# Inter-chunk output of a Mamba-2 scan: from a scaled PSUM product to C multiplied by the decays on GpSimd, accumulated in place

## The chip, the cores and the metric

The kernel runs on one core of a Trainium2 chip. The metric is the device time of one execution in microseconds; three runs of the kernel before took 2874.92, 2874.94 and 2874.92 us (median 2874.92). Five engines work side by side, each through its own queue in program order: PE (matmuls), DVE (vector), ACT (scalar activations), POOL (GpSimd) and SP (which here only issues transfers). Matmuls write PSUM; DVE and ACT read PSUM and write SBUF.

## What is computed

One layer of a hybrid decoder on 256 prompt tokens and 64 sample tokens (T = 320 columns): a SwiGLU feed-forward block, a token mixer, and a second feed-forward block. The mixer holds a state-space scan in chunks of 128 tokens, and the change is inside it:

```
cum      = cumsum(dt * A)                       # per chunk and head
y_diag   = (C B^T * exp(cum_t - cum_s) * dt) x  # within a chunk
h_start  = state at the chunk's start           # chunk 0: zero; chunk 1: from chunk 0
y_off[t] = exp(cum_t) * (C_t . h_start)         # from the earlier chunk
y        = y_diag + y_off + D * x
```

There are 32 heads of 64 channels in four groups of eight; a group shares B and C (128 states). The prompt has two chunks, so y_off exists for tokens 128 to 255 alone. The state at the prompt's end, exp(cum_end) * h_start plus chunk 1's own sum, is an output too (o_hp). The mixer further has a 31-tap depthwise convolution with a layer norm, three kinds of gates on the projection's columns, a norm over the scan's output and two output projections.

## The kernel before, in words

**The main stream.** Every dense layer goes through `phase` (line 328). Weights stream from HBM in tiles of 128 x 512 (a chunk holds four 128 x 128 blocks). Each is split into a high part on ACT (wh) and a low part on DVE (wl), and each block takes three matmuls of 320 columns: wh by the high input, wl by the high input, wh by the low input. The input projection's second part, `WIN_2`, has 40 groups of two column blocks; a group runs 32 block steps, so 96 matmuls, into two PSUM banks named acc. There are four such banks. `WIN_PLAN` (line 50) gives the kind of each group: eight "x" groups feed the scan, "z" groups gate its output, "gcc" and "gssd" groups are gates, "glu" groups feed the 31-tap convolution. When a group ends, a small task reads its two banks out and thereby frees them.

**What orders the rest.** All side work is written as Python generators that a planner interleaves with the main stream while the program is built; the queues then execute in the order that came out. One tick is two block steps, so six main matmuls. At each tick `step_bg` (line 296) lets generators go on while its estimates of the DVE and ACT clocks are less than 1.4 us ahead of its PE clock. A generator says `yield n` to sleep n ticks; LAG is 5. If the main stream needs a PSUM bank that is not free, `force` (line 306) moves the tasks and the generators of priority below 3, without regard to sleeping, and with no main matmul written in between, until the bank is free.

**The scan.** `ssd` (line 815) goes through the four groups. For a group it transposes x and B, makes `xdt` (x times dt) and `xw` (x times the decays to the chunk's end), the masked product of B and C (`cbm`), and `s0`, the state after chunk 0. Then (lines 1013 to 1027) it waits LAG ticks, takes two banks named m (there are three), multiplies C by s0 on PE into one bank and sums chunk 1's state into the other; DVE scales the first by exp(cum) into `yo1`, scales s0 by the chunk's decay, adds the sum, and POOL stores s0 to o_hp.

Next come two halves of four heads; a half is called a pair p, 0 to 7. `load_w` has broadcast the pair's cum rows from a DRAM scratch, `cumd`, to all partitions of `wd` (two buffers: one in tile eu, one in the last four slices of x). The generator waits until 12 ticks after that load was issued; ACT subtracts (12 Relu activations of 128 or 64 columns) and takes the exponential, DVE multiplies by cbm, and LAG + 3 ticks later PE forms y for the pair in two m banks: xdt by wd for three token blocks, plus yo1 by the identity for chunk 1, plus the sample part by a selection matrix. DVE adds D * x, y is ready, and `load_w(p + 2)` is issued LAG ticks later.

**What waits for the scan.** After the last pair of group 3 and the few instructions behind it, the generator says "ypath" (line 1087). `gate1` (line 1197) for blocks 12 to 15 and `gate2` (line 1202) hold back until then, since they write where wd and the scan's tiles lie: the two "gcc" groups behind the "z" groups, groups 29 and 30 of 40, leave their four acc banks occupied until "ypath". `sst` (line 920) updates the sample states, 32 tiles h0, and has POOL store each to o_hs; `conv31` (line 1092) runs the long convolution on DVE and at the end of each of eight channel blocks has POOL store a pad tile and load the next into the same buffer.

In the profile all PE, DVE and ACT instructions have the helper's line, L78, so they are told apart by their tiles. There fu holds xdt, s0 and yo1; gu holds xw; eu holds cbm, the transposed B and one wd; x is the other wd; hu and xb the sample state's inputs; bc is B and C; cw the constants with the identity. PE in 32-bit floating point shows two instructions for one matmul of the program.

Of the kernel before, what the change touches and what calls it, by code (L numbers as in the profile page):

```python
# [6 lines left out]
F32 = mybir.dt.float32  # L7
F32R = mybir.dt.float32r
AF = mybir.ActivationFunctionType
ALU = mybir.AluOpType  # L10
# [13 lines left out]
LAG = 5  # L24
# [145 lines left out]
class Builder:  # L170
# [432 lines left out]
    def mixer(self, on_k):  # L603
        nc, io = self.nc, self.io
# [10 lines left out]
        ident, ones = self.ident, self.ones  # L615
# [85 lines left out]
        ec1 = self.sp.tile([128, 32], F32, name="ec1", tag="ec1")  # L701
# [4 lines left out]
        def dt_gen(a):  # L706
            du = unit("du", "E")
            v = lambda i: du[0:32, i, :]
            V = nc.vector
# [26 lines left out]
            for i, cst in enumerate((13, 11, 9, 7, 5, 3)):  # L736
                V.scalar_tensor_tensor(v(1), v(1), 1.0 / cst, v(3), op0=ALU.add, op1=ALU.mult)
                if i % 3 == 2:
# [11 lines left out]
            cum, ec, dw = v(5), v(6), v(7)  # L750
# [9 lines left out]
            yield 1  # L760
            V.tensor_tensor(dw, dw, v(4), op=ALU.mult)
            nc.sync.dma_start(out=self.cumd, in_=cum)
            nc.scalar.activation(stg.rearrange("p (j i) -> p j i", i=32)[:, :, 0:16],
                                 ec[:, 256:320].rearrange("p (j i) -> p j i", i=16), AF.Copy)
            d1 = v(0)[:, 0:32]
# [18 lines left out]
            for e in range(2):  # L784
                nc.tensor.matmul(b2.ap[64 * e : 64 * e + 64, 64:192],
                                 lhsT=self.par[:, e : e + 1].to_broadcast([32, 64]),
                                 rhs=v(1)[:, 0:128], start=True, stop=True)
# [27 lines left out]
        def ssd():  # L815
# [6 lines left out]
            ef, ff, gf, hf = (q.rearrange("p a b -> p (a b)") for q in (eu, fu, gu, hu))  # L822
            wds = (eu[:, 0:4], self.x[:, 12:16])
            btok = ef[:, 1280:1664]
            cbm = ef[:, 1664:1984]
            yos = ef[:, 1984:2496]
            xdt = ff[:, 0:1536].rearrange("p (c f) -> p c f", c=3)
            s0 = ff[:, 1536:2048]
            yo1 = ff[:, 2048:2560]
            xw = gf[:, 0:1024].rearrange("p (c f) -> p c f", c=2)  # L830
            xws = gf[0:64, 1024:1536]
            xss = hf[0:96, 0:1024].rearrange("p (q f) -> p q f", q=2)
# [3 lines left out]
            V = nc.vector  # L836
            hd = lambda ap: ap.rearrange("p (h q) -> p h q", q=64)
            BLK = ((0, 0, 128), (1, 128, 128), (2, 256, 64))
            at = {}
            h0s = {}  # L840

            def tbc(i, c, g, n=128):
                return tk[0:n, i, c, 8 * g : 8 * g + 8].unsqueeze(2).to_broadcast([n, 8, 64])
# [12 lines left out]
            def load_w(p):  # L856
                if p < 8:
                    nc.sync.dma_start(out=wds[p % 2],
                                      in_=self.cumd[4 * p : 4 * p + 4].partition_broadcast(128))
                    at["w", p] = self.tick  # L860

            def load_h0(i):
                if i < 32:
                    g, q, jj = i // 8, i // 4 % 2, i % 4
                    h = self.hp.tile([128, 512], F32, name="h0", tag="h0")
                    nc.sync.dma_start(out=h, in_=io["h0"][4 * g + jj, q])
                    h0s[i] = h
                    at["h", i] = self.tick
# [80 lines left out]

            bhl = self.sp.tile([64, 2, 128], F32R, name="bhl", tag="bhl")  # L950
            load_w(0)
            assert "spilled" in self.ready
            load_w(1)
            self.spawn(sst_all(), 2.5)
            for i in range(3):
                load_h0(i)
            self.spawn(ysamp(), 1.5)
            for g in range(4):
# [3 lines left out]
                B, C = Bt(g), Ct(g)  # L962

                def xT(c):
                    _, t0, n = BLK[c]
                    b = self.ring("m")
                    for i in range(4):
                        nc.tensor.transpose(b.ap[0:n, 128 * i : 128 * i + 128], XS(4 * g + i)[:, t0 : t0 + n], ident)
                    return b
# [9 lines left out]
                b0, b1 = xT(0), xT(1)  # L979
# [7 lines left out]
                b0 = xT(2)  # L987
                b1 = self.ring("m")
# [10 lines left out]
                b0 = self.ring("m")  # L999
                b1 = self.ring("m")  # L1000
                nc.tensor.matmul(b1.ap, lhsT=btok[:, 0:128], rhs=xw[:, 0], start=True, stop=True)
                for c, t0, n in BLK:
                    nc.tensor.matmul(b0.ap[0:n, t0 : t0 + n], lhsT=B[:, t0 : t0 + n], rhs=C[:, t0 : t0 + n],
                                     start=True, stop=True)
# [3 lines left out]
                                op=ALU.mult)  # L1008
# [1 line left out]
                b0.free = True  # L1010
                nc.scalar.activation(s0, b1.ap, AF.Copy)
                b1.free = True
                yield LAG
                while not self.can("m", 2):
                    yield 1
                b0 = self.ring("m")
                b1 = self.ring("m")
                nc.tensor.matmul(b1.ap, lhsT=btok[:, 128:256], rhs=xw[:, 1], start=True, stop=True)
                nc.tensor.matmul(b0.ap, lhsT=C[:, 128:256], rhs=s0, start=True, stop=True)
                yield 1  # L1020
                V.tensor_tensor(hd(yo1), hd(b0.ap), tbc(2, 1, g), op=ALU.mult)
                b0.free = True
                V.tensor_tensor(hd(s0), hd(s0), ec1[:, 8 * g : 8 * g + 8].unsqueeze(2).to_broadcast([128, 8, 64]),
                                op=ALU.mult)
                V.tensor_tensor(s0, s0, b1.ap, op=ALU.add)
                b1.free = True
                nc.gpsimd.dma_start(out=io["o_hp"][g], in_=s0)
                yield 0
                for half in range(2):
                    p = 2 * g + half  # L1030
                    wd = wds[p % 2]
                    while ("w", p) not in at or self.tick < at["w", p] + 12:
                        yield 1
                    for i in range(4):
                        h = 4 * p + i
                        for c, t0, n in BLK:
                            nc.scalar.activation(wd[0:n, i, t0 : t0 + n], wd[0:n, i, t0 : t0 + n], AF.Relu,
                                                 bias=tk[0:n, 0, c, h : h + 1], scale=-1.0)
                        yield 0
                    nc.scalar.activation(wd[:, :, 0:256], wd[:, :, 0:256], AF.Exp, scale=-1.0)  # L1040
                    nc.scalar.activation(wd[0:64, :, 256:320], wd[0:64, :, 256:320], AF.Exp, scale=-1.0)
                    yield 2
                    V.tensor_tensor(wd[:, :, 0:256], wd[:, :, 0:256],
                                    cbm[:, 0:256].unsqueeze(1).to_broadcast([128, 4, 256]), op=ALU.mult)
                    V.tensor_tensor(wd[0:64, :, 256:320], wd[0:64, :, 256:320],
                                    cbm[0:64, 256:320].unsqueeze(1).to_broadcast([64, 4, 64]), op=ALU.mult)
                    yield LAG + 3
                    while ("yos", g) not in self.ready or not self.can("m", 2):
                        yield 1
                    bb = []  # L1050
                    for jj in range(2):
                        b = self.ring("m")
                        bb.append(b)
                        co = [(2 * half + jj) * 128 + 64 * e for e in range(2)]
                        for c, t0, n in BLK:
                            for e in range(2):
                                nc.tensor.matmul(b.ap[64 * e : 64 * e + 64, t0 : t0 + n],
                                                 lhsT=xdt[0:n, c, co[e] : co[e] + 64],
                                                 rhs=wd[0:n, 2 * jj + e, t0 : t0 + n],
                                                 start=True, stop=(c == 0))  # L1060
                            if c == 0:
                                continue
                            src, mat = (yo1, ident) if c == 1 else (yos, self.r2)
                            for e in range(2):
                                nc.tensor.matmul(b.ap[64 * e : 64 * e + 64, t0 : t0 + n],
                                                 lhsT=src[:, co[e] : co[e] + 64], rhs=mat[:, 0:n],
                                                 start=False, stop=True)
                    self.later(LAG, lambda n=p + 2: load_w(n))
                    yield 1
                    for jj in range(2):  # L1070
                        j = 4 * g + 2 * half + jj
                        b = bb[jj]
                        V.scalar_tensor_tensor(XS(j), XS(j), self.col("dd", j), b.ap[:, :T], op0=ALU.mult, op1=ALU.add)
                        b.free = True
                        self.ready.add(("y", j))
                self.ready.add(("yos_used", g))
                nc.scalar.activation(xwh, xws, AF.Copy)
                nc.scalar.activation(bhl[:, 0], btok[0:64, 256:384], AF.Copy)
                yield 1
# [300 lines left out]
    def run(self):  # L1380
        nc, io, tc = self.nc, self.io, self.tc
        from contextlib import ExitStack
        with ExitStack() as ctx:
# [12 lines left out]
            dp = P("dp", 1, space=bass.MemoryType.DRAM)  # L1396
# [11 lines left out]
            self.dummy, self.negA = small[:, 0:2], small[:, 2:3]  # L1408
            self.sd = dp.tile([4, 64, 1280], F32, name="sd")
            self.cumd = dp.tile([32, T], F32, name="cumd")  # L1410
            self.xd = dp.tile([128, KT, T], F32, name="xd")
            self.xgen = 0
            nc.vector.memset(self.ones, 1.0)
# [25 lines left out]
            g = lambda nm: (lambda k: self.col(nm, k))  # L1439
# [32 lines left out]
            for k in range(KT):  # L1472
                xk = self.x[:, k]
                t = self.temp()
# [146 lines left out]
```

## Time and profile before

| what | value |
|---|---|
| median of three runs | 2874.92 us |
| the profiled execution's own time | 2875.14 us |
| its span, first to last instruction | 2873.1 us |
| PE busy | 2861.5 us (100%) |
| DVE busy | 1710.0 us (60%) |
| ACT busy | 1336.0 us (46%) |
| POOL busy | 40.0 us (1%) |
| granted TensorE clock | 0.999 |

A group of instructions is one row: engine, operation, output tile and input tiles, shape, count, then busy time, mean length of one in ns, and the idle time before them with what ended it. A timeline row has start and length in us, and in brackets the idle time before it and its releaser. Matmuls overlap in such rows, so their cost on PE is the distance of starts, not the length. A row of the windows has length, busy time of PE with the count, granted clock, busy share of the DMA engines and GB/s.

### The profile page before, as it was taken

Reading aid. Unit: us, or ns where it says so; the run is one execution under the profiler, and the core shown is the slowest. Engines: PE = TensorE matmul, PEld = TensorE weight load, DVE = VectorE, ACT = ScalarE, POOL = GpSimd, SP = SyncE. Lnnn points to the kernel's source line nnn. Section 1 sums busy time; section 2 is a strip of 40 time slices with the busy share of each in tenths; the row PEclk is TensorE's granted clock in tenths of the full one; section 3 lists DMA queues with packets and bytes.
Section 4 is the critical chain, followed back from the end, with each engine's and each line's share of the span. In section 5 each row is a group of like instructions: output and inputs, shape, how many; then the busy total and the mean of one; then the engine's idle time right before and its main releaser. Section 6 shows DMA issues by size and latency. Waiting matters only on the chain.

```text
span 2873.1 us, 50758 instructions
## 1 busy us (share of the span) xinstructions
PE 2861.5 (100%) x19655; PEld 2831.8 (99%) x19655; DVE 1710.0 (60%) x3375; ACT 1336.0 (46%) x2499; POOL 40.0 (1%) x79
## 2 busy tenths in 40 slices
PE   9999999999999999999999999999999999999998
PEld 9999999999999999999999999999999999999998
DVE  6555433555544887588989987557555434555544
ACT  6444433444444566456554544455444433444443
POOL 0000000000000000000000000000000000000000
PEclk9999999999999999999999999999999999999999
DMA  6444444444444545665566645544444444444443
GB/s 205 148 152 149 149 152 148 153 149 150 151 148 153 175 149 191 212 223 190 179 198 224 203 147 167 171 133 148 153 148 151 151 148 153 147 152 150 149 153 118
DMA packets 132882, 465.86 MB, mean 162 GB/s; under 512 B 15488, under 2 KB 17312, under 8 KB 132640
## 3 DMA queue, kind: packets, MB, share of 16 engines
q1 hardware_dynamic: 127024, 442.43, 48.8%
q0 software_dynamic: 5472, 20.18, 2.0%
q8 instruction: 154, 2.52, 0.4%
q14 instruction: 88, 0.72, 0.1%
q10 hardware_dynamic: 144, 0.01, 0.0%
HBM read 443.77 MB, written 18.78 MB: 161 GB/s over the span
## 4 chain that ended last, share of the span: by engine, by line
PE 99%; DVE 1%; DMA 0%; ACT 0%; issue 0%; SPq 0%; ACTq 0%
PE acc L78 93%; PE m L78 5%; PE n L78 1%; DVE t L78 0%; DMA raw<-w_up1a 0%; DVE x L78 0%; DMA x<-x 0%; ACT L78 0%; ACT wh L78 0%; ACT xgh L78 0%; DVE xgl L78 0%; DVE st L78 0%; SPq L210 0%; DVE wl L78 0%; ACT t L78 0%
## 5 line engine op out<-in xcount | busy, mean ns | idle before, releaser
L78 DVE TENSOR_TENSOR wl<-raw,wh 128x512 fp32r<-128x512 f32 (+1 forms) x1569 | 1080.9, 690 | 1104.7 <-PE acc L78 974.0
L78 ACT ACTIVATE wh<-raw 128x512 fp32r<-128x512 f32 (+1 forms) x1569 | 987.4, 631 | 1463.6 <-PE acc L78 1388.3
L78 PE MATMUL acc<-xgh,wh 128*128 128x320 f32 x4240 | 1316.5, 310 | 1.9 <-ACT xgh L78 1.9
L78 PE MATMUL acc<-xgl,wh 128*128 128x320 f32 x4240 | 1310.8, 309 | 0.5 <-DVE xgl L78 0.5
L78 PE MATMUL acc<-xgh,wl 128*128 128x320 f32 x4240 | 1310.8, 309 | 0.0
L78 PEld LDWEIGHTS acc<-xgh,wh 128*128 128x128 f32 x4240 | 796.9, 188 | 8.0 <-issue 3.7
L78 PEld LDWEIGHTS acc<-xgh,wl 128*128 128x128 f32 x4240 | 796.9, 188 | 2.7 <-issue 1.0
L78 PEld LDWEIGHTS acc<-xgl,wh 128*128 128x128 f32 x4240 | 796.8, 188 | 1.3 <-DVE xgl L78 1.3
L78 PE MATMUL acc<-hl,wh 128*128 128x320 f32 x1408 | 435.1, 309 | 0.0
L78 PE MATMUL acc<-hh,wl 128*128 128x320 f32 x1408 | 435.1, 309 | 0.0
L78 PE MATMUL acc<-hh,wh 128*128 128x320 f32 x1408 | 435.1, 309 | 0.0
L78 PEld LDWEIGHTS acc<-hh,wl 128*128 128x128 f32 x1408 | 264.3, 188 | 0.0
L78 PEld LDWEIGHTS acc<-hh,wh 128*128 128x128 f32 x1408 | 264.3, 188 | 0.0
L78 PEld LDWEIGHTS acc<-hl,wh 128*128 128x128 f32 x1408 | 264.3, 188 | 0.0
L78 DVE SCALAR_TENSOR_TENSOR cvo<-pad,cw,cvo 128x256 f32<-128x256 f32 x480 | 152.3, 376 | 0.0
L78 DVE TENSOR_TENSOR t<-acc,rb 128x320 f32<-128x320 f32 x212 | 93.9, 482 | 2.1 <-ACT rb L78 2.1
L78 PE MATMUL acc<-ch,wh 128*128 128x320 f32 x256 | 79.1, 309 | 0.0
L78 PE MATMUL acc<-ch,wl 128*128 128x320 f32 x256 | 79.1, 309 | 0.0
L78 PE MATMUL acc<-cl,wh 128*128 128x320 f32 x256 | 79.1, 309 | 0.0
L78 PE MATMUL m<-xgh,wl 128*128 128x320 f32 x240 | 74.3, 310 | 0.3 <-DVE wl L78 0.3
L78 PE MATMUL m<-xgh,wh 128*128 128x320 f32 x240 | 74.5, 311 | 0.0
L78 PE MATMUL m<-xgl,wh 128*128 128x320 f32 x240 | 74.2, 309 | 0.0
(210 smaller groups left out, 1583.5 us busy)
## 6 DMA issues: line engine op xcount, KB each, us to landing
raw<-w_in SPq DMA_DIRECT2D x176, 512.0 KB, 3.7
raw<-w_up1b SPq DMA_DIRECT2D x88, 512.0 KB, 3.5
raw<-w_up2a SPq DMA_DIRECT2D x88, 512.0 KB, 3.5
raw<-w_up2b SPq DMA_DIRECT2D x88, 512.0 KB, 3.5
raw<-w_up1a SPq DMA_DIRECT2D x85, 512.0 KB, 3.5
raw<-w_dn1a SPq DMA_DIRECT2D x44, 512.0 KB, 3.5
raw<-w_dn1b SPq DMA_DIRECT2D x44, 512.0 KB, 3.5
raw<-w_dn2a SPq DMA_DIRECT2D x44, 512.0 KB, 3.5
```

Of the source, the lines that this page charges most:

```text
L78: return f(*a, **k)
```

## The change

The product of C and the state is no longer formed on its own. exp(cum) for chunk 1 is written to a second DRAM scratch, `ecd`; per pair, `load_e` broadcasts its four rows to all partitions of `ce` (128 x 512, in the place of yo1, one buffer), and GpSimd multiplies them in place by C. In y's accumulation s0 is now the weights and ce the moving operand, where yo1 was the weights and the identity moved. `load_e(p + 1)` is issued LAG ticks behind pair p's matmuls, and the half's start waits for both loads, each 12 ticks old. The matmul of C and s0, DVE's scaling into yo1 and the waits around them go away; the scaling of s0, chunk 1's sum and the store to o_hp move behind the group's two halves.

```diff
@@ dt_gen
             nc.sync.dma_start(out=self.cumd, in_=cum)
+            nc.sync.dma_start(out=self.ecd, in_=ec[:, 128:256])
@@ ssd
-            yo1 = ff[:, 2048:2560]
+            ce = ff[:, 2048:2560].rearrange("p (h t) -> p h t", h=4)
...
+            def load_e(p):
+                if p < 8:
+                    nc.sync.dma_start(out=ce, in_=self.ecd[4 * p : 4 * p + 4].partition_broadcast(128))
+                    at["e", p] = self.tick
...
             load_w(0)
+            load_e(0)
...
                 nc.scalar.activation(s0, b1.ap, AF.Copy)
                 b1.free = True
-                yield LAG
-                while not self.can("m", 2):
-                    yield 1
-                b0 = self.ring("m")
-                b1 = self.ring("m")
-                nc.tensor.matmul(b1.ap, lhsT=btok[:, 128:256], rhs=xw[:, 1], start=True, stop=True)
-                nc.tensor.matmul(b0.ap, lhsT=C[:, 128:256], rhs=s0, start=True, stop=True)
-                yield 1
-                V.tensor_tensor(hd(yo1), hd(b0.ap), tbc(2, 1, g), op=ALU.mult)
-                b0.free = True
-                V.tensor_tensor(hd(s0), hd(s0), ec1[:, 8 * g : 8 * g + 8].unsqueeze(2).to_broadcast([128, 8, 64]),
-                                op=ALU.mult)
-                V.tensor_tensor(s0, s0, b1.ap, op=ALU.add)
-                b1.free = True
-                nc.gpsimd.dma_start(out=io["o_hp"][g], in_=s0)
                 yield 0
                 for half in range(2):
                     p = 2 * g + half
                     wd = wds[p % 2]
-                    while ("w", p) not in at or self.tick < at["w", p] + 12:
+                    while any((i, p) not in at or self.tick < at[i, p] + 12 for i in "ew"):
                         yield 1
+                    nc.gpsimd.tensor_tensor(ce, ce, C[:, 128:256].unsqueeze(1).to_broadcast([128, 4, 128]),
+                                            op=ALU.mult)
...
-                            src, mat = (yo1, ident) if c == 1 else (yos, self.r2)
                             for e in range(2):
+                                src, mat = (s0, ce[:, 2 * jj + e]) if c == 1 else (yos, self.r2)
...
                     self.later(LAG, lambda n=p + 2: load_w(n))
+                    self.later(LAG, lambda n=p + 1: load_e(n))
...
                 self.ready.add(("yos_used", g))
+                V.tensor_tensor(hd(s0), hd(s0), ec1[:, 8 * g : 8 * g + 8].unsqueeze(2).to_broadcast([128, 8, 64]),
+                                op=ALU.mult)
+                while not self.can("m"):
+                    yield 1
+                b1 = self.ring("m")
+                nc.tensor.matmul(b1.ap, lhsT=btok[:, 128:256], rhs=xw[:, 1], start=True, stop=True)
+                yield 1
+                V.tensor_tensor(s0, s0, b1.ap, op=ALU.add)
+                b1.free = True
+                nc.gpsimd.dma_start(out=io["o_hp"][g], in_=s0)
```

Since the planner decides the order, the diff does not tell where things come to stand. Three places at the scan's end, on which the prediction rests:

PE at the last pair's y, before (m banks receive y; x is wd, fu is xdt and yo1, cw the identity and the selection, eu the sample part; acc rows are the main stream):

```order
L78 MATMUL acc<-xgl,wh 128x320
L78 MATMUL m_15969<-x,fu 64x128 x4
L78 MATMUL m_15969<-cw,fu 64x128 x2
L78 MATMUL m_15969<-x,fu 64x64 x2
L78 MATMUL m_15969<-cw,eu 64x64 x2
L78 MATMUL m_15980<-x,fu 64x128 x4
L78 MATMUL m_15980<-cw,fu 64x128 x2
L78 MATMUL m_15980<-x,fu 64x64 x2
L78 MATMUL m_15980<-cw,eu 64x64 x2
L78 MATMUL acc<-xgh,wh 128x320
```

Hundreds of acc rows stand before and behind. The same place on PE in the changed program (hu is a sample state product, "fu" alone is s0 by ce, n the sum of squares of the scan's gated output, gu by eu chunk 1's state sum):

```order
L78 MATMUL m_16363<-hu 128x512
L78 MATMUL m_16365<-x,fu 64x128 x4
L78 MATMUL m_16365<-fu 64x128 x2
L78 MATMUL m_16365<-x,fu 64x64 x2
L78 MATMUL m_16365<-cw,eu 64x64 x2
L78 MATMUL m_16376<-x,fu 64x128 x4
L78 MATMUL m_16376<-fu 64x128 x2
L78 MATMUL m_16376<-x,fu 64x64 x2
L78 MATMUL m_16376<-cw,eu 64x64 x2
L78 MATMUL n<-ones,acc_sq 128x1 x3
L78 MATMUL m_16418<-gu,eu 128x512
L78 MATMUL acc<-xgh,wh 128x320
```

The last pair's y has moved 225 rows back in PE's order, nearly all of them main matmuls. It now stands at the end of a group's main matmuls (group 30 of 40), and between it, the n rows and the state sum no acc row is left.

DVE right behind the last pair's y, before (xs<-...m takes y out of PSUM, wl is the weights' low part, hu and bhl the group's last two instructions ahead of "ypath", cvo the long convolution):

```order
L78 SCALAR_TENSOR_TENSOR xs_9863<-xs_9863,cw,m_15969 128x320
L78 SCALAR_TENSOR_TENSOR xs_9863<-xs_9863,cw,m_15980 128x320
L78 TENSOR_TENSOR wl<-raw,wh 128x512
L78 TENSOR_TENSOR hu<-gu,hu 64x512
L78 TENSOR_TENSOR bhl<-eu,bhl 64x128
L78 TENSOR_TENSOR wl<-raw,wh 128x512
L78 SCALAR_TENSOR_TENSOR cvo<-pad,cw,cvo 128x256
L78 SCALAR_TENSOR_TENSOR cvo<-pad,cw,cvo 128x64
```

And in the changed program, from behind the two rows that take y out (fu<-fu,ec scales s0, xs<-xs,t is the z gate, acc_sq adds the squares, st is the norm's 1/sqrt, fu<-fu,m adds the state sum, x<-acc,rb reads out the four acc banks of the two "gcc" groups):

```order
L78 TENSOR_TENSOR fu<-fu,ec_9877 128x512
L78 TENSOR_TENSOR xs_9864<-xs_9864,t 128x320 x2
L78 TENSOR_TENSOR acc_sq<-acc_sq,t 128x320 x2
L78 TENSOR_SCALAR st<-n 128x3
L78 RECIPROCAL st<-st 128x3
L78 SCALAR_TENSOR_TENSOR st<-st 128x3
L78 TENSOR_TENSOR st<-st 128x3
L78 SCALAR_TENSOR_TENSOR st<-st 128x3
L78 TENSOR_TENSOR fu<-fu,m_16418 128x512
L78 TENSOR_TENSOR hu<-gu,hu 64x512
L78 TENSOR_TENSOR bhl<-eu,bhl 64x128
L78 TENSOR_TENSOR x<-acc,rb 128x320 x4
```

The read-out of the four banks now stands behind this whole row of small steps, with no weight split and no convolution between them.

POOL at the same place in the changed program (fu<-fu,bc is the last pair's product; pad the convolution's tile, h the sample states):

```order
L949 DMA o_hs<-h_15921 128x512
L949 DMA o_hs<-h_16161 128x512
L1122 DMA o_pad<-pad 128x590
L640 DMA pad<-pad 128x590
L1026 TENSOR_TENSOR fu<-fu,bc 128x512
L949 DMA o_hs<-h_16300 128x512
L1081 DMA o_hp<-fu 128x512
```

Before, POOL had no computing here, only stores and pad loads; now the last product stands behind a pad's store and its reload.

More of the change, by code (lines that the diff above doesn't have):

```diff
@@ L1410, in run @@
             self.cumd = dp.tile([32, T], F32, name="cumd")
+            self.ecd = dp.tile([32, 128], F32, name="ecd")
             self.xd = dp.tile([128, KT, T], F32, name="xd")
```

## Prediction, made blind

> **What bounds the kernel now.** I read the page's busy times and its chain first, then what PE waited for.
>
> ```profile
> span 2873.1 us, 50758 instructions
> PE 2861.5 (100%) x19655; PEld 2831.8 (99%) x19655; DVE 1710.0 (60%) x3375; ACT 1336.0 (46%) x2499; POOL 40.0 (1%) x79
> PE 99%; DVE 1%; DMA 0%; ACT 0%; issue 0%; SPq 0%; ACTq 0%
> PE acc L78 <- ACT xgh L78: 1.9, 3, 1.5
> ```
>
> PE is busy over the whole span, the chain runs along PE for 99%, and the largest entry in the table of PE's waits is 1.9 us in all. So whatever leaves PE's queue shortens the time by its full cost, nothing on the other engines counts while it stays hidden, and a hole in PE's stream counts in full. Two questions follow: what do PE's removed matmuls cost, and does the new order leave holes?
>
> **What PE is spared.** Per group one matmul of C by s0 goes, 128 x 512; the count of small y matmuls stays, since s0 by ce replaces yo1 by the identity with equal shapes (64 x 128 in the order). The price is in the timeline of PE at the last group:
>
> ```profile
> 1408.82 1.02 PE L78 MATMUL m<-gu,eu 128*128 128x512 f32 x2
> 1409.67 1.02 PE L78 MATMUL m<-fu,bc 128*128 128x512 f32 x2
> 1410.13 0.71 PE L78 MATMUL acc<-xgh,wh 128*128 128x320 f32 x1
> 1410.68 0.31 PE L78 MATMUL acc<-xgh,wl 128*128 128x320 f32 x1
> 1410.82 0.31 PE L78 MATMUL acc<-xgl,wh 128*128 128x320 f32 x1
> ```
>
> From 1408.82 to 1410.68 stand two such matmuls and one main matmul. Main matmuls start 0.147 us apart (1410.68, 1410.82, and so on), so one removed matmul is (1.86 - 0.147) / 2 = 0.86 us; four are **3.4 us**. Bounds: 0.85 by the first two starts, 0.93 if the whole 1.86 is shared; 3.4 to 3.7.
>
> **What lies beside PE.** DVE loses four scalings of 0.68 us. POOL gains eight products, SP eight loads of 256 KB and one store of 16 KB.
>
> ```profile
> L78 DVE TENSOR_TENSOR fu<-m,tk 128x512 f32<-128x512 f32 x12 | 8.2, 683 | 0.0
> L1481 POOL TENSOR_TENSOR x<-x,t 128x320 f32<-128x320 f32 x6 | 5.0, 865 | 1053.6 <-DVE t L78 1052.7 <-ACT x L78 0.9
> x<-cumd SPq DMA_DIRECT2D x4, 640.0 KB, 5.9
> h<-h SPq DMA_DIRECT2D x32, 256.0 KB, 4.5
> ACT wh L78 <- DMA raw<-w_in: 6.8, 4, 2.4
> ```
>
> A product of 512 columns isn't shown. Its bounds are 0.87 (the 320 columns' row, all fixed) and 1.38 (scaled by 512/320); I take 1.4. A ce load lands in 4.5 to 5.9 us, while the generator waits 12 ticks, 12 x 6 x 0.147 = 10.6 us. Then 12 Relu steps, the exponential and LAG + 3 ticks pass before PE needs the product, at least 10 ticks or 8.8 us; so for pairs 1 to 7 load and product cost nothing. Without cover it would be up to 7.3 us a pair. The weight stream hardly waits for its transfers (6.8 us in all, none of which reached PE), so eight more loads cost nothing either; uncovered, 8 x 4.5 = 36 us.
>
> **What comes later.** ce has one buffer. load_e(p + 1) comes LAG ticks behind pair p's matmuls and is waited for 12 more: 17 ticks, 15 us, between a group's halves, where wd with two buffers let the next half begin at once. Removing LAG and the bank waits ahead of the halves gives back some 6 ticks a group. The order nets it: the last pair's y stands 225 rows later, 225 x 0.147 = 33 us. Is there room for that?
>
> ```profile
> 1458.20 0.28 DVE L78 TENSOR_TENSOR bhl<-eu,bhl 64x128 fp32r<-64x128 f32 x1
> 1477.54 0.88 DVE L78 TENSOR_TENSOR x<-acc,rb 128x320 f32<-128x320 f32 x2
> 1491.38 0.88 DVE L78 TENSOR_TENSOR x<-acc,rb 128x320 f32<-128x320 f32 x2
> ```
>
> "ypath" comes LAG ticks (4.4 us) behind bhl, so at 1462.9. The two "gcc" groups end at about 1476 and 1490 and are read out at once. Were "ypath" not there by 1490, all four acc banks would be held and PE would stop. The slack is 27 us, and the shift 33. The order agrees: at the end of group 30 the planner was forced, and writes the last pair's half, the z gates, the norm's first part and the group's end with no main matmul between. **PE must wait there for a chain across the engines.** Everything behind the first y matmul on PE is queued behind it, and ACT's and DVE's weight splits wait for PE in turn.
>
> I count from T0, when PE has finished group 30. Up to y:
>
> ```profile
> 1471.35 0.63 ACT L78 ACTIVATE wh<-raw 128x512 fp32r<-128x512 f32 x1 [1.14 <-PE acc L78]
> 1473.10 0.63 ACT L78 ACTIVATE wh<-raw 128x512 fp32r<-128x512 f32 x1 [1.11 <-PE acc L78]
> L78 ACT ACTIVATE cvo<-pad,cw 128x256 f32<-128x256 f32 x8 | 4.7, 588 | 0.3 <-DVE pad L78 0.3
> L78 ACT ACTIVATE cvo<-pad,cw 128x64 f32<-128x64 f32 x8 | 3.4, 428 | 0.0
> 1436.52 1.75 ACT L78 ACTIVATE x<-x,tk 128x128 f32<-128x128 f32 x6
> 1440.15 1.28 ACT L78 ACT_TABLE_LOAD   x1
> 1441.45 1.37 ACT L78 ACTIVATE x<-x 128x1024 f32<-128x1024 f32 x2
> 1444.78 1.54 DVE L78 TENSOR_TENSOR x<-x,eu 128x1024 f32<-128x1024 f32 x2
> ```
>
> ACT can't run ahead: its splits come 1.75 us apart, released by PE. The last one starts some 1.6 before T0; with 0.63 and the convolution's 0.59 and 0.43 ACT is at the Relu steps at T0 + 0.05. Twelve are 2 x 1.75, the table 1.28, the exponentials 1.37: T0 + 6.2. DVE's product takes 1.54, its first part some 1.2: y can start at T0 + 7.4. POOL's way there:
>
> ```profile
> 1341.41 0.54 POOL L943 DMA_DIRECT2D o_hs<-h  x1 [17.87 <-DVE h L78]
> ...
> 1346.68 0.54 POOL L640 DMA_DIRECT2D pad<-pad  x1 [4.20 <-DMA o_pad<-pad]
> ...
> 1487.93 0.54 POOL L640 DMA_DIRECT2D pad<-pad  x1 [16.16 <-ACT cvo L78]
> ```
>
> In the order the last product stands behind o_hs, o_pad and the pad's reload, which waits for the store to land: 5.8 us from o_hs to the reload's end. With o_hs at about T0 and the product's 1.4 it is there at T0 + 7.2, just not last. Then y and the rest:
>
> ```profile
> 1452.14 0.66 PE L78 MATMUL m<-x,fu 128*64 128x128 f32 x8
> ...
> 1454.66 0.41 PE L78 MATMUL acc<-xgh,wh 128*128 128x320 f32 x1
> L78 DVE SCALAR_TENSOR_TENSOR xs<-xs,cw,m 128x320 f32<-128x320 f32 x16 | 8.1, 537 | 1.4 <-PE m L78 1.4
> 1464.53 0.89 DVE L78 TENSOR_TENSOR xs<-xs,t 128x320 f32<-128x320 f32 x2
> 1466.36 0.82 ACT L78 ACTIVATE t<-xs 128x320 f32<-128x320 f32 x2
> 2856.58 0.72 PE L78 MATMUL n<-ones,acc_sq 128*128 128x1 f32 x6
> 1474.49 0.16 DVE L78 TENSOR_SCALAR st<-n 128x3 f32<-128x3 f32 x1 [0.82 <-PE n L78]
> 1475.67 0.16 DVE L78 SCALAR_TENSOR_TENSOR st<-st 128x3 f32<-128x3 f32 x1
> ```
>
> y took 2.5 us of PE (1452.14 to 1454.66). After 7 us of idleness I take 3.8, between 2.5 and twice that (the clock, below): T0 + 11.2. On DVE: 0.54 to take y out, 0.68 to scale s0, 0.88 for the two z gates, 0.45 for the second square, 0.49 to add it; 0.7 for n on PE; 1.34 for the st steps with the square root on ACT between (1474.49 to 1475.83); then at 0.69, 0.68, 0.28 and 0.48 state sum, hu, bhl and the first bank. PE goes on at **T0 + 18.4**. Of that it would have worked 4.1 anyway (y 2.5, n 0.7, state sum 0.86): **14.3 us idle**.
>
> **The clock after the hole.** The trace shows two places where PE comes out of or falls into idleness:
>
> ```profile
> 5.45 0.47 PE L78 MATMUL acc<-xgh,wh 128*128 128x320 f32 x1
> 5.72 0.47 PE L78 MATMUL acc<-xgh,wl 128*128 128x320 f32 x1
> ...
> 2866.00:2869.00 3.00, 0.62 (x2) 0.71 0.88 339
> 2869.00:2873.10 4.10, 0.00 (x0) 0.50 0.40 147
> ```
>
> At the beginning main matmuls start 0.27 us apart instead of 0.147, until about 6.8; at the end the granted clock falls to 0.71 and 0.50. A restart at that pace loses between nothing and 45% of the 5.7 us that the start took, 2.6; I take **1.8**, nearer the start's row, as few matmuls run inside the hole. The Trainium skill, "TensorE: Matmul & The Clock Gate", Part 1, says that an idle window of about 3.4 us halves the clock and that about 3.4 us of activity restores it. By it the restart would lose 1.5 instead of 1.8 and the sum be 2887.3; the start's row lasted longer than that rule, the end's agrees.
>
> **The sum.** -3.4 + 14.3 + 1.8 = +12.7 on the profiled execution's 2875.14 (2.0 of it outside the span) gives 2887.8; the median is 0.2 below that execution, so **2887.6 us**. Low end: y at full clock (-1.3), DVE steps overlapping as their starts do (-1.0), no loss at the restart (-1.8): 2883.5. High end: y at half clock (+1.2), twelve hand-overs of 0.15 (+1.8), POOL 2 late, restart 2.6 (+0.8): 2893.4.
>
> **Rivals.**
>
> *The cover holds.* The hole is filled or never opens and only the removal counts: 2874.9 - 3.4 = 2871.5. For it: the slack of 27 us is near the shift of 33, and PE waits nowhere now. Against: PE's order has no filler, and PE can't pass a waiting matmul. 7%. It decides as soon as "ypath" is written ahead of group 30's end.
>
> *POOL comes last.* The pad's reload waited 16.2 us once (1487.93), for the convolution's readers. If that happens behind the last o_pad, the product comes at T0 + 19 instead of 7.2; from T0 + 7.9 on, when PE has the four xdt matmuls behind it, each us late is a us lost: 11 more, 2899. Against: in the order the convolution's last step on that pad stands ahead of the half. 9%.
>
> *DVE and POOL exclude each other.* DVE's product of wd and cbm and POOL's of ce and C read two SBUF inputs each at nearly the same time, T0 + 6 to 7.4. If one holds the other off for its length, 1.4 us come on top: 2889.0. No row shows two such instructions side by side here. 18%. The Trainium skill, "SBUF — State Buffer", section "SBUF: two separate sides", has it so: DVE and GpSimd share one port pair, and whichever starts first holds it for its whole instruction, a DVE one with two SBUF inputs against a GpSimd one that reads SBUF; no run here shows it.
>
> The forecast itself has 62% (2883.5 to 2893.4). 4% are left for holes at other pairs (2%, slower) and for a gain above 5.7 us (2%). About 0.2%, 5.7 us, is what can be told from no change here. Slower by more: 62 + 18 + 9 + 2 = 0.91, of which I hold back 0.01; within: 0.08; faster: 0.02. The range of 8 in 10 is the forecast's own with the exclusion and some width for unread waits: 2881 to 2896.
>
> **What would show it.** PE's waits should hold one place near 1490 us with some 14 us of idleness, in two or three pieces: the longest, about 7, ahead of the last y, ended by DVE's product; then some 2 to 4 ahead of n; then some 4 ahead of the main stream, ended by the first x<-acc,rb. Elsewhere no new PE wait. The groups should lack m<-fu,bc and show POOL's product at 0.9 to 1.4 us. It is wrong if PE shows no such hole, if POOL's product ends the first piece, or if holes stand at other pairs too.

## The result: 17 us slower, and where they lie

| kernel | median | runs | ratio to the kernel before, 95% interval |
|---|---|---|---|
| before | 2874.93 us | 6 | |
| changed | 2891.95 us (2891.28 to 2892.69) | 6 | 1.0059 [1.0049, 1.0069] |

The forecast was 2887.6 us, in 2881 to 2896. The direction, the place and the mechanism came as forecast; the loss is 17.0 us instead of 12.7.

First the page of the changed kernel: span, busy times, and the group of POOL's products.

```profile
span 2890.2 us, 50773 instructions
PE 2865.1 (99%) x19647; PEld 2834.0 (98%) x19647; DVE 1716.4 (59%) x3371; ACT 1338.1 (46%) x2501; POOL 52.1 (2%) x87
L1026 POOL TENSOR_TENSOR fu<-fu,bc 128x512 f32<-128x512 f32 x8 | 11.7, 1468 | 136.0 <-DMA fu<-ecd 129.7 <-PE acc L78 6.3
```

The span grew by 17.1 us and PE's busy time by only 3.6: the rest is new idleness. The table of PE's waits (who waited, for whom, us in total, times, longest) says where:

```profile
PE m L78 <- issue: 7.8, 1, 7.8
PE n L78 <- DVE acc_sq L78: 3.3, 1, 3.3
PE acc L78 <- DVE x L78: 2.0, 1, 2.0
PE acc L78 <- ACT xgh L78: 1.7, 3, 1.3
```

Three waits that the kernel before doesn't have, each once, 13.0 us; the last row has its like before. They stand in one place. PE's timeline there, without the main matmuls between:

```profile
1483.14 0.39 PE L78 MATMUL m<-hu 96*128 96x512 f32 x1
1491.29 1.12 PE L78 MATMUL m<-x,fu 128*64 128x128 f32 x8 [7.76 <-issue]
...
1495.22 0.34 PE L78 MATMUL m<-cw,eu 128*64 128x64 f32 x4
1498.84 1.44 PE L78 MATMUL n<-ones,acc_sq 128*128 128x1 f32 x6 [3.28 <-DVE acc_sq L78]
1500.14 2.05 PE L78 MATMUL m<-gu,eu 128*128 128x512 f32 x2
1504.17 0.64 PE L78 MATMUL acc<-xgh,wh 128*128 128x320 f32 x1 [1.98 <-DVE x L78]
```

T0, the end of PE's last work of group 30, is 1483.53. y starts at T0 + 7.8, the sum of squares at T0 + 15.3, and the main stream at T0 + 20.6. The view has "issue" for what ended the first wait; that it was DVE's product of wd and cbm follows from DVE's row below and from the run noprod. The same stretch on DVE and POOL:

```profile
1488.72 2.80 DVE L78 TENSOR_TENSOR x<-x,eu 128x1024 f32<-128x1024 f32 x2 [6.53 <-ACT x L78]
...
1502.23 0.69 DVE L78 TENSOR_TENSOR fu<-fu,m 128x512 f32<-128x512 f32 x1 [0.71 <-PE m L78]
1488.83 1.27 POOL L1026 TENSOR_TENSOR fu<-fu,bc 128x512 f32<-128x512 f32 x1
```

Two things are to be seen. DVE's product of wd and cbm took 2.80 us where it took 1.54 before, and POOL's product, 1.27, lies inside it: 1.54 + 1.27 = 2.81. And the state sum on PE took 2.05, so that DVE waited for it (0.71) before it could go on to the bank read-out. Windows over the hole (stretch, length, busy time of PE, weight loads, DVE, ACT and POOL, then the granted clock, DMA share and GB/s) show why:

```profile
1483.60:1488.20 4.60, 0.00 (x0) 0.00 (x0) 0.00 (x0) 4.57 (x13) 0.00 (x0) 1.00 1.03 324
1488.30:1495.10 6.80, 3.81 (x36) 3.06 (x36) 4.38 (x7) 0.69 (x2) 2.37 (x3) 0.50 0.62 137
1495.10:1498.50 3.40, 0.46 (x8) 0.25 (x6) 2.65 (x6) 1.29 (x3) 0.00 (x0) 1.00 0.26 87
1498.60:1508.70 10.10, 7.88 (x25) 6.31 (x26) 5.38 (x15) 6.84 (x15) 0.54 (x1) 0.50 0.23 61
1508.60:1512.00 3.40, 3.40 (x24) 3.40 (x24) 0.95 (x2) 0.82 (x2) 0.00 (x0) 0.98 0.45 154
```

The clock falls 4.7 us into the first wait and is whole again for one stretch of 3.4 us, in which PE has hardly any work. So nearly everything that PE does between the first wait and 1508.6 runs at half the clock: y but for its last matmuls, the sum of squares, the state sum and then the first 17 main matmuls. The changes lie 6.8, 3.4 and 10.2 us apart, whole multiples of 3.4. Laid side by side with the kernel before, the k-th main matmul of each, the changed kernel is 0.4 us late from the program's start on, 6.9 early at the end of group 30, 14.1 late at the next main matmul, 16.3 late 17 matmuls on, and 17.0 late at the end.

### The profile page after: what moved, and what is told of

Same layout as the page of the kernel before. It is cut to its first block, busy times and chain, and to the rows that moved or that the text cites. A ratio compares the mean times of both kernels' runs of the same rounds, so it can differ in the third digit from the quotient of the medians.

```text
span 2890.2 us, 50773 instructions
## 1 busy us (share of the span) xinstructions
PE 2865.1 (99%) x19647; PEld 2834.0 (98%) x19647; DVE 1716.4 (59%) x3371; ACT 1338.1 (46%) x2501; POOL 52.1 (2%) x87
## 4 chain that ended last, share of the span: by engine, by line
PE 98%; DVE 1%; issue 0%; DMA 0%; ACT 0%; SPq 0%; ACTq 0%; DVEq 0%
PE acc L78 92%; PE m L78 5%; PE n L78 1%; DVE t L78 0%; DVE x L78 0%; DMA raw<-w_up1a 0%; DMA x<-x 0%; DVE fu L78 0%; ACT L78 0%; ACT wh L78 0%; ACT t L78 0%; ACT xgh L78 0%; DVE acc_sq L78 0%; DVE xs L78 0%; DVE xgl L78 0%
```

## The experiments

### The same change with a shorter wait (wait6)

```diff
-                    while any((i, p) not in at or self.tick < at[i, p] + 12 for i in "ew"):
+                    while any((i, p) not in at or self.tick < at[i, p] + n for i, n in (("e", 6), ("w", 12))):
```

> The changed kernel with one number different: a half waits until 6 ticks behind the ce load instead of 12 (the wait behind wd's load stays 12). In the order the last pair's y then stands ahead of group 30's last matmuls and no stretch without main matmuls is left. Theory (the time is lost only because the last y comes too late for the four acc banks): the hole near 1483 us is gone and only the four removed products count, 2874.9 - 3.4 = 2871.5 us (2870.5 to 2873). Rival (the GpSimd products, their eight loads and the exclusion with DVE cost time in every group): the loss stays for the greater part, 2885 us or more. A middle result, 2875 to 2880, would say that the load, given 6 ticks, 5.3 us, is now itself waited for.

Measured: 2878.98 us against 2875.16, ratio 1.0013 [1.0004, 1.0022]. 13 of the 17 us are gone, with all products and loads of ce still there, so the second rival falls. But the hole isn't closed. PE's waits:

```profile
PE acc L78 <- DVE x L78: 1.9, 1, 1.9
PE n L78 <- DVE acc_sq L78: 1.6, 1, 1.6
```

PE's y came in time, and what waits now is the tail on DVE: y taken out, gates, squares, the norm's small steps, then the bank read-out. PE waits nowhere for a ce load. My middle result had the wrong reason, and my reading of the order was wrong too: in the trace the state sum, the sum of squares and one m<-hu stand between group 30's last main matmul (1484.82) and the next (1491.26), with no main matmul among them. The restart at half pace came with it: the main matmuls behind this hole start 0.27 us apart for some 3.8 us. The clock had fallen at 1488.1, between the two waits:

```profile
1484.70:1488.00 3.30, 1.66 (x9) 0.83 (x8) 3.06 (x7) 2.00 (x5) 0.00 (x0) 1.00 0.89 299
1488.10:1491.20 3.10, 1.22 (x5) 0.71 (x4) 2.17 (x10) 2.82 (x5) 0.54 (x1) 0.50 0.26 100
```

So the first wait, of 1.6 us, was enough for it.

### The old kernel, made late (late14, late6, late4)

```diff
-                    while ("w", p) not in at or self.tick < at["w", p] + 12:
+                    while ("w", p) not in at or self.tick < max(at["w", p] + 12, at.get("y", 0) + 14):
...
+                    at["y"] = self.tick
                     self.later(LAG, lambda n=p + 2: load_w(n))
```

> The kernel before, with no ce, no GpSimd product and the old order inside a group, but each half held back until 14 ticks after the previous pair's y matmuls. In the order the last y then stands at group 30's end as in the changed kernel, with the long convolution's and sample states' first steps instead of the state sum in the stretch without main matmuls. Theory (lateness alone makes the hole): by the steps measured in the changed kernel, 1.3 for four sample activations, 3.4 Relu, 1.3 table, 1.4 exponential and 1.2 DVE bring y to 8 us after the group's end, y 4.3 and the gates to the first bank read-out some 4 more, 16 in all; of these 3.7 would be worked anyway, so 12 idle and 2 for the restart: 2889 us (2886 to 2891). Rival (the hole comes from the GpSimd product and its load): 2874.9.

> As the kernel before, with each half held back until 6 ticks after the previous pair's y matmuls: the last y stands 187 PE rows later than before but still ahead of the end of group 30, and no stretch without main matmuls is left. Theory (a threshold: lateness costs nothing until the four acc banks are held): 2874.9 us, within 2.5. Rival (every pair's delay costs time, about in proportion to the shift): with 187 of some 225 rows about 12 us more, 2887.

> The kernel before, each half held back until 4 ticks after the previous pair's y matmuls: the last y stands 52 rows later and ypath 10 ticks, 9 us, later, still well ahead of group 30's end. With 6 ticks the loss was about 2 to 4 us, with 14 it was 16. Theory (a threshold: the slack of some 25 us must be used up first): no difference, 2875.2 us within 0.7. Rival (each tick of delay costs): about 1 to 2 us more.

| delay behind the previous y | last y, PE rows later | median | ratio |
|---|---|---|---|
| 4 ticks | 52 | 2875.09 us | 0.9997 [0.9988, 1.0007] |
| 6 ticks | 187 | 2878.94 us | 1.0013 [1.0004, 1.0022] |
| 14 ticks | some 230, at group 30's end | 2891.45 us | 1.0057 [1.0043, 1.0071] |

The kernel of 14 ticks has no ce, no product on POOL and all four products of C and s0, and loses 16.3 us. Its waits:

```profile
PE m L78 <- ACT hu L78: 4.5, 1, 4.5
PE m L78 <- issue: 3.9, 1, 3.9
PE acc L78 <- DVE x L78: 3.6, 1, 3.6
```

Their sum is 12.0, as expected. The measured 2891.45 lies 2.45 us above my figure of 2889 and just outside my range. The step that I had wrong is the beginning of ACT's row of steps ahead of y: its four sample activations waited for a transfer and began 3.1 us behind the group's end, and not at once:

```profile
1488.91 1.28 ACT L78 ACTIVATE hu<-xb,cw 96x128 fp32r<-96x128 f32 x4 [4.16 <-DMA xb<-sd]
1490.24 1.65 PE L78 MATMUL m<-hu 96*128 96x512 f32 x3 [4.45 <-ACT hu L78]
```

The table load of 1.3 us that I had counted isn't there. So y began 10.0 us behind the group's end where I had 8. The half clock is here too: the three m<-hu take 1.65 us and y 4.5, where they take 0.7 and 2.7 in the kernel before; for y I had counted 4.3. So lateness alone makes a hole. 4 ticks cost nothing (in the trace the scan takes as long as before within 0.1 us), 6 cost 3.8 us by the medians and 14 cost 16.3. That is a threshold, somewhere between a shift of 52 rows and one of 187, and no price per tick. At 6 ticks I expected nothing and was wrong: its trace has waits of 1.1 us ahead of n and 0.7 ahead of the main stream. That kernel's runs spread from 2876.8 to 2880.4, more than the others', and its profiled one was the shortest, so what the longer ones add is in no trace.

### What the four products cost (twice)

```diff
                 nc.tensor.matmul(b0.ap, lhsT=C[:, 128:256], rhs=s0, start=True, stop=True)
+                nc.tensor._e.matmul(b0.ap, lhsT=C[:, 128:256], rhs=s0, start=True, stop=True)
```

(`_e` is the engine without the planner's clock, so the order of all else stays.)

> The kernel before with the product of C and s0 written twice into the same bank in each of the four groups (same output). It prices what the change removed. By the starts in the timeline: 4 x 0.86 = 3.4 us more, 2878.3 us. By the whole distance of 1.86 for two: 3.7. Rival (such matmuls fall into slots that PE has anyway): 0, 2874.9.

Measured: 2878.41 us, ratio 1.0010 [1.0001, 1.0019], 3.3 us more. PE's timeline at the last group, the added matmul at L1020:

```profile
1411.09 1.02 PE L78 MATMUL m<-gu,eu 128*128 128x512 f32 x2
1411.95 1.02 PE L78 MATMUL m<-fu,bc 128*128 128x512 f32 x2
1412.81 1.02 PE L1020 MATMUL m<-fu,bc 128*128 128x512 f32 x2
```

The starts are 0.86 apart, and the main stream is 3.4 us later behind the four groups than ahead of them. The term is right, and nothing of it is hidden.

### DVE and POOL (noprod)

```diff
-                    nc.gpsimd.tensor_tensor(ce, ce, C[:, 128:256].unsqueeze(1).to_broadcast([128, 4, 128]),
-                                            op=ALU.mult)
```

> The changed kernel without the GpSimd product: ce holds the decays alone, so the part of y from the earlier chunk leaves out C. Order and loads stay. In the changed kernel's trace DVE's product of wd and cbm took 2.80 us at the last pair and 1.54 at the others, and GpSimd's product of 1.27 us ran meanwhile. Theory (the two exclude each other): DVE's product takes 1.54 again, y starts 1.26 earlier, and the time is 2892.0 - 1.3 = 2890.7 us. Rival (2.80 has another cause, such as waiting for the second exponential, or y waits for another thing anyway): 2892.0.

Measured: 2890.61 us, ratio 1.0052 [1.0038, 1.0066]. The interval can't tell 1.3 us from nothing; the trace can:

```profile
1488.41 1.55 DVE L78 TENSOR_TENSOR x<-x,eu 128x1024 f32<-128x1024 f32 x2 [6.53 <-ACT x L78]
```

```profile
1482.83 0.39 PE L78 MATMUL m<-hu 96*128 96x512 f32 x1
1489.74 1.12 PE L78 MATMUL m<-x,fu 128*64 128x128 f32 x8 [6.52 <-issue]
```

DVE starts after the same wait for ACT, 6.53, and takes 1.55 again; y starts 1.24 earlier, counted from T0, and the main stream 1.05. The exclusion is shown by taking one of the two away. In the changed kernel itself it is seen at other places too, in both directions (the timelines of POOL and DVE around two products):

```profile
1185.05 1.29 POOL L1026 TENSOR_TENSOR fu<-fu,bc 128x512 f32<-128x512 f32 x1 [48.09 <-DMA fu<-ecd]
1185.62 1.27 DVE L78 TENSOR_TENSOR wl<-raw,wh 128x512 fp32r<-128x512 f32 x1 [1.07 <-PE acc L78]
1220.58 1.87 POOL L1026 TENSOR_TENSOR fu<-fu,bc 128x512 f32<-128x512 f32 x1 [6.28 <-PE acc L78]
```

A split of 0.69 us that met a running product ended 0.55 behind the product's end, after 1.27; and a product on POOL that DVE's instructions were ahead of took 1.87 instead of 1.27. At those pairs DVE isn't waited for, so it costs nothing. The Trainium skill, "SBUF — State Buffer", section "SBUF: two separate sides", says that the two share a port pair which one instruction holds to its end. These rows agree with it.

### The clock inside the hole (warm)

```diff
                         bb.append(b)
+                        if p == 7 and jj == 0:
+                            self.filler = (btok[:, 128:256], xw[:, 1])
+                            for _ in range(8):
+                                nc.tensor._e.matmul(b.ap, lhsT=self.filler[0], rhs=self.filler[1], start=True, stop=True)
...
-    def rstd_a(self, srcs, scale, fill=None):
+    def rstd_a(self, srcs, scale, fill=None, warm=False):
         nc = self.nc
         b = self.ring("n")
+        for _ in range(3 if warm else 0):
+            nc.tensor._e.matmul(b.ap, lhsT=self.filler[0], rhs=self.filler[1], start=True, stop=True)
...
-            r = self.rstd_a([self.acc_s], 1.0 / D)
+            r = self.rstd_a([self.acc_s], 1.0 / D, warm=True)
```

> The changed kernel with matmuls of no use put into the waits of the hole: eight of 128x512 into y's bank ahead of the last y (8 x 0.86 = 6.9 us, inside the wait of 7.8) and three into n's bank ahead of n (2.6, inside 3.3). They are overwritten. Theory (PE's clock falls because PE idles, and the slow matmuls in the hole lie on the path): y takes 2.5 us instead of 4.3, n and state sum 0.7 less each on the path, and the main stream starts at full pace, 1.9 less: 2892.0 - 5.1 = 2886.9 us. Rival (the clock falls for another reason, or the chain over DVE hides PE's pace): 2892.0, or up to 2 more where a filler matmul delays y.

Measured: 2888.30 us, ratio 1.0044 [1.0030, 1.0057]: 3.7 us better than the changed kernel, not 5.1. (The two ran beside different executions of the kernel before; against its own each, and in the traces, it is 4.1.)

```profile
1490.89 0.66 PE L78 MATMUL m<-x,fu 128*64 128x128 f32 x8 [0.63 <-DVE x L78]
...
1493.14 0.34 PE L78 MATMUL m<-cw,eu 128*64 128x64 f32 x4
1493.40 2.84 PE L390 MATMUL n<-gu,eu 128*128 128x512 f32 x6
1496.75 0.83 PE L78 MATMUL n<-ones,acc_sq 128*128 128x1 f32 x6 [0.51 <-DVE acc_sq L78]
1497.44 1.10 PE L78 MATMUL m<-gu,eu 128*128 128x512 f32 x2
1500.67 0.63 PE L78 MATMUL acc<-xgh,wh 128*128 128x320 f32 x1 [2.12 <-DVE x L78]
```

y takes 2.6 us instead of 4.3, the state sum 1.1 instead of 2.05, and from y's end to the main stream 7.2 pass instead of 8.6. That 7.2 is what the prediction had counted from its rows, which were all taken at the full clock. What I hadn't expected: the clock fell again at 1500.3, inside the last wait of 2.1 us, and the main stream's start is at half pace in this kernel too. In the 3.4 us ahead of that fall PE was busy for 1.65:

```profile
1490.90:1493.40 2.50, 2.50 (x40) 1.96 (x40) 1.85 (x6) 0.00 (x0) 0.58 (x1) 1.00 0.06 18
1496.90:1500.30 3.40, 1.65 (x8) 0.82 (x8) 2.31 (x9) 2.65 (x9) 0.54 (x1) 1.00 0.22 78
1500.60:1503.80 3.20, 3.13 (x12) 3.13 (x13) 1.81 (x5) 2.87 (x6) 0.00 (x0) 0.51 0.69 184
```

Since the filler matmuls change nothing but PE's being busy, that the clock follows PE's activity is shown.

### The change without the lateness (early)

```diff
-                    while any((i, p) not in at or self.tick < at[i, p] + 12 for i in "ew"):
+                    while any((i, p) not in at or self.tick < at[i, p] + n for i, n in (("e", 5), ("w", 12))):
...
-                    self.later(LAG, lambda n=p + 1: load_e(n))
+                    self.later(2, lambda n=p + 1: load_e(n))
```

> The changed kernel with load_e issued 2 ticks behind the pair's matmuls instead of 5, and the half waiting 5 ticks behind it instead of 12. In the order the last y stands 178 rows ahead of where the change has it, and ypath comes some 12 us ahead of group 30's end; with the wait of 6 ticks alone 1.6 and 1.9 us of waiting and the slow restart were left, since DVE's small steps still stood ahead of the bank read-out. Theory (lateness is the whole loss): no wait at group 30, and only the four products' 3.4 us count: 2875.2 - 3.4 = 2871.8 us. Rival (the ce loads and GpSimd products have a price of their own, hidden in the hole so far; or the load is now waited for, up to 8 times some 1 to 2 us): 2875 or more.

Measured: 2873.64 us against 2875.41, ratio 0.9993 [0.9985, 1.0002]. The hole is gone: none of the three waits is left, and PE has no wait for a ce load. So all of the hole was lateness. The interval can't tell the gain from nothing; in the traces, from the scan's beginning to its end, it is 1.5 us, and that isn't 3.4. PE waits nowhere for what is missing, so it is in PE's own work. Sorting what stands between main matmuls in the two traces shows one difference beside the four products: ysamp's two sets of eight matmuls into n, which stood together in the kernel before, stand apart in six of eight cases. First the kernel before, then the early one:

```profile
1146.81 0.31 PE L78 MATMUL acc<-xgl,wh 128*128 128x320 f32 x1
1147.05 0.64 PE L78 MATMUL n<-gu,cblk 128*32 128x256 f32 x8
1147.51 0.61 PE L78 MATMUL n<-cvo,cblk 128*32 128x256 f32 x8
1148.05 0.42 PE L78 MATMUL acc<-xgh,wh 128*128 128x320 f32 x1
1148.30 0.31 PE L78 MATMUL acc<-xgh,wl 128*128 128x320 f32 x1
```

```profile
1144.17 0.31 PE L78 MATMUL acc<-xgl,wh 128*128 128x320 f32 x1
1144.41 0.64 PE L78 MATMUL n<-gu,cblk 128*32 128x256 f32 x8
1144.97 0.41 PE L78 MATMUL acc<-xgh,wh 128*128 128x320 f32 x1
1145.23 0.31 PE L78 MATMUL acc<-xgh,wl 128*128 128x320 f32 x1
```

From the last main matmul ahead to the second behind, less two distances of 0.147: 1.20 us for both sets together, 0.77 for one alone. Two alone cost 1.54, so parting the two sets costs 0.34 a time, six times 2.0. It is no price of every break of the main stream: counted in the same way, the state sum alone costs 0.86 and together with the product of C and s0 1.72, twice that; and where both ysamp sets stand right beside another group of 1.76, the whole costs 2.96, their plain sum.

### The breaks mended (pairs)

```diff
-                        while ("t", 4 * g + r) not in at or self.tick < at["t", 4 * g + r] + 10:
+                        r1 = 4 * g + (r | 1)
+                        while ("t", r1) not in at or self.tick < at["t", r1] + 10:
```

> The kernel of the run with the early load (load_e 2 ticks behind the matmuls, wait of 5), and one more edit: ysamp, the generator of the sample tokens' part of y, waits at each even r until the state tiles of r and r + 1 are both there, so that its two sets of eight 128x256 matmuls into n stand behind one another again. In the kernel before a stretch of main matmuls is broken once for the two, and the break costs 1.20 us; in the early kernel they stand apart in six of eight cases and cost 0.77 each, so 0.34 more a time. Theory (each break of the main stream has its own price of 0.34 us, and that is what ate half of the four products' gain): six breaks fewer, 6 x 0.34 = 2.0 us below the early kernel, 3.4 below the kernel before: 2871.8 us. Rival (the eight ce loads and products keep the other half): no change against the early kernel, 1.8 below the kernel before.

> The early-load kernel once more, beside the run with the paired sample products on the same chip. Both theories: 1.8 us below the kernel before, as measured (2873.6 where the kernel before took 2875.4).

Measured on one chip: 2872.31 us for this kernel, ratio 0.9990 [0.9981, 0.9999], and 2874.04, 0.9996 [0.9987, 1.0005], for the early one again, which is 1.2 us below the kernel before and not 1.8. By the medians the six partings cost 1.7 us, and this kernel is 2.9 below the kernel before. In its trace all eight pairs stand together again, 1.20 each, and from the scan's beginning to its end the main stream gains 3.3 us on the kernel before, nearly the four products' 3.4; the early kernel gains 1.5 in both of its traces. So the six partings cost 1.8 in the traces, 0.31 each, and for the eight loads and products hardly anything is left. That the price belongs to these two sets and not to every break is read from the rows above; why they share something when they stand together is open. This version is the fastest of all, though by 0.1%, hardly more than its interval.

## Why the prediction was right, and where its sum was short

- **What PE is spared, 3.4:** right; doubling gave 3.4 in the trace.
- **Load and product cost nothing for pairs 1 to 7:** right for the waits; the early kernel, with everything of ce in place, has none, and the pairs kernel gains all but 0.1 of the 3.4.
- **The slack of 27 us and the shift of 33:** right. In the old kernel a shift of 187 rows, 27 us, loses 3.8 us and one of 52 rows nothing, and 14 ticks lose nearly as much as the whole change.
- **The hole, main stream at T0 + 18.4:** measured T0 + 20.6. This is the term that was mis-sized, in two steps. "y can start at T0 + 7.4" came out at 7.8: ACT's Relu steps began 0.6 earlier than I had them, and the excluded product, 1.3, came on top; that the two nearly cancelled is luck. The 3.8 that I took for y came out at 4.3 and the 0.7 for n at 1.4, and the state sum on PE, which I had let run beside DVE's small steps, took 2.05, so that DVE waited for it: I had priced the half clock for y in part and for the two others not at all. y's end to the main stream grew from 7.2 to 8.6; the warm kernel, at the full clock, gives 7.2.
- **The clock after the hole, 1.8:** 2.2 from the first main matmul to the 18th. The Trainium skill's page, "TensorE: Matmul & The Clock Gate", Part 1, gives some 3.4 us of activity for a restart and an idle window of that length for the fall. Here the half pace lasted 4.4 us behind this hole and 3.0 in the warm kernel, and the clock fell in waits shorter than that: in the 3.4 us ahead of the fall PE had been busy for 1.65 in the warm kernel, and in the 3.3 ahead of it for 1.66 in the one with the wait of 6. The prediction's "the end's agrees" was misread too: in the kernel before the last matmul ended at 2866.6, and the clock fell at 2867.2. The measured rows decide.
- **A term that was missing:** the new order parts four of the eight pairs of ysamp's matmuls in the changed kernel, 4 x 0.34 = 1.4 us. I counted the change's own matmuls and not how the rest of the scan lies between the main matmuls.
- **The rest:** 0.4 us at the very beginning of the profiled program, before anything of the change runs. With 2.2 for the hole, 0.4 for the restart and 1.4 for the partings this is the 4.4 us between 2887.6 and the profiled execution's 2892.0.
- **The rivals:** "the cover holds" fell. "POOL comes last" fell: its product ended at 1490.10, 1.4 us before DVE's. "DVE and POOL exclude each other" was true, at 1.27 us, and went together with the forecast. I had it as another outcome with 18%, though nothing in it speaks against the forecast's steps.
- **What would show it:** the hole stood in one place in three pieces, 7.8, 3.3 and 2.0, for 7, 2 to 4 and 4. The third is shorter because n and the state sum, at half pace, fill it. POOL's products had a mean of 1.47 us, above the 0.9 to 1.4 named, since DVE held some of them off.

## What to carry to other kernels

Work that is moved later costs nothing until it passes the point where something else needs it, and then the whole chain behind it lies open at once: count the slack to that point before you weigh what is saved, and if a single buffer has made a loop slow, shorten its wait before you give the change up. Price the steps in such a hole at the clock that PE has there, not at the clock of the rows they were taken from. And where a planner decides the order, look at what the rest of the program does too: groups of matmuls that stood together can come to stand apart, and here that took about half of what the change saves.

## What the runs showed of the hardware

- A product on POOL (128 x 512, 32 bits, two inputs) takes 1.27 us alone, and DVE instructions with two inputs stand still for it: 2.80 for 1.54, 1.27 for 0.69. Held off by DVE it takes 1.87, once 2.09.
- PE's clock fell to one half in waits much shorter than the first hole: inside one of 2.1 us in the warm kernel, 1.8 us after its beginning, and behind one of 1.6 us in the kernel with the wait of 6. With waits of 1.1 and 0.7 us (late6) the granted clock of the profiled run stayed whole.
- Two sets of eight 32-bit matmuls (128 x 256, 32 output rows each) into one bank cost PE 1.20 us when they stand together between main matmuls and 0.77 each when they stand apart, although PE shows no wait there. A 128 x 512 product in 32 bits costs 0.86 either way.
